# One pool for all 4 KB tiles, decay matrices per head, and another order of the mixing's steps

## The chip, the cores and the metric

The kernel runs on one core of a Trainium2 chip. The metric is the device time of one execution in microseconds. The engines are TensorE (PE in the profile; PEld is its weight load), VectorE (DVE), ScalarE (ACT), GpSimd (POOL) and SyncE (SP), which here issues all DMAs. Each engine takes its instructions in the order in which the program gives them.

## The reference

Two layers work on 256 latent and 256 context tokens of width 1024. Each layer is a half-step feed-forward, a token mixing, and another half-step feed-forward, each with a modulated norm before it and a modulated residual behind it. Cut to what matters:

```python
for l in range(DEPTH):                                    # 2
    m = split(silu(c) @ w_mod[l] + b_mod[l], 9)           # and mc from c_ctx
    x  = x  + 0.5 * m[2]  * swiglu(modulate(rms_norm(x),  m[0],  m[1]),  ffn1_w_in[l], ffn1_w_out[l])
    xc = xc + 0.5 * mc[2] * swiglu(...)                   # the context, same weights
    y, y_ctx = token_mixing(...)                          # w_in: 1024 -> 2560, three head groups
    x  = x  + m[5] * (y @ w_out[l])
    x  = x  + 0.5 * m[8] * swiglu(..., ffn2_w_in[l], ffn2_w_out[l])
    # context likewise, in the first layer alone
# token_mixing: A neighbourhood attention, 8 heads of 32, one softmax over window and context keys
#               B retention, 4 heads, q and k of 64, v of 128, both directions, decay per direction
#               C diagonal complex state-space scan, 16 groups of 64 states, both directions, GELU, GLU
```

All is float32. The result must agree with float32 products, so a product of two float32 matrices is made from three products of a rounded part (hi) and a rest (lo).

## The kernel before

Activations lie transposed, 128 features by 512 tokens (context first), eight tiles `x`. A weight comes by DMA into a 4 KB tile `raw` (128 x 1024); ScalarE rounds it into `whi`, VectorE subtracts into `wlo` (`unit`), and three matmuls per pair of tiles collect into a PSUM bank (`mm3`). A feed-forward goes through 22 blocks of hidden features in four parts. Its projections, and those of the mixing, are bound to nothing but weights and the normalised input `hhi`, `hlo`.

The mixing (`mixing`) makes the projection `ub` and then steps three generators: `s` is the state-space group (`s5`: products `s5z`, work on VectorE and GpSimd, products `s5y`), `a` the attention (`attention`: values `va`, then for each half of four heads the projections `qk` and their norm, copies that stack hi and lo parts into `qs` and `ks`, and for each token tile and head the score matmul `sc`, a maximum `mx` on VectorE, the exponential `p` on ScalarE, transposes `pt`, their copy `pts`, and the products `ot`), and `r` the retention (`retention`, `ret_head`: projections `rqk`, values `vb`, gates `rgate`, products `rab`, `rot`, `rsb`). The string `ORDER` says in which order the steps are recorded.

The program is then ordered by a planner in the file itself (`Sched.run`): each engine takes the recorded instruction of the lowest number that can start by the planner's own times, if its output tile has a free slot and no older work would be left without one (`fits`). So the number of slots of each pool and the recorded order decide which matmuls stand between a score matmul and its transposes. Names may have a limit on tiles in use (`LIMITS`: two `sc`, two `pt`).

Slots before: 55 pages of 2 KB (`page`), and 4 KB tiles by kind: three `raw`, two `whi`, two `wlo`, two `wmod` (weights of the modulation, whose rows VectorE multiplies with the row `crow` of the condition), four `ptab` (tables of the scan). The rows `crow` stay for the whole program. `h` and the mixed `y` take pages for hi and lo.

Of the kernel before, what the change touches and what calls it, by code (L numbers as in the profile page):

```python
# [21 lines left out]
ND = D // 128  # L22
# [157 lines left out]
class Sched:  # L180
# [28 lines left out]
    def record(self, eng, key, method, a, k):  # L209
# [315 lines left out]
class Block:  # L525
    NPAGES, NRAW, NHI, NLO, NMOD, AHEAD, NEAR, MODNEAR, FIRST, MOD, TAB, CUT = 55, 3, 2, 2, 2, 1000, 250, 700, 300, 0, 900, 2
    ORDER = ["saar" + "sar" * 4 + "ra" + "sar" * 4 + "g" + "rrr",
             "saar" + "sar" * 2 + "sr" * 2 + "ra" + "sar" * 2 + "sr" * 2 + "g" + "rrr"]
# [4 lines left out]
    LIMITS = dict(s5z=1, s5y=1, sc=2, pt=2, glu=2, nabias=2, rkt=1, rab=1, qs=4, ks=4)  # L533

    def __init__(self, tc, ctx, I, O):
# [14 lines left out]
        tagged(wp, "raw", self.NRAW)  # L550
        tagged(wp, "whi", self.NHI)
        tagged(wp, "wlo", self.NLO)
        tagged(wp, "ptab", 4)
        tagged(wp, "wmod", self.NMOD)
# [4 lines left out]
    def page(self, name, dtype=F32):  # L559
        return self.limited(self.nc.tile("page", [128, 512], dtype, name))  # L560

# [22 lines left out]
    def raw(self, src, n=1024):  # L584
        t = self.nc.tile("raw", [128, 1024], F32, "raw")
# [3 lines left out]
    def unit(self, src, n=1024, w=128, pages=False, at=None):  # L589
# [5 lines left out]
        for o in range(0, n, 512) if pages else (0,):  # L595
            if pages:
                m, t = 512, [self.page("raw"), self.page("whi", F32R), self.page("wlo", F32R)]
            else:
                m = n
                t = [nc.tile(x, [128, 1024], y, x) for x, y in (("raw", F32), ("whi", F32R), ("wlo", F32R))]  # L600
            r, hi, lo = [x[:, :m] for x in t]
# [21 lines left out]
    def begin(self):  # L623
# [11 lines left out]
        nc.vector.memset(self.ones, 1.0)  # L635
        self.mhalf = self.keep([128, 64], "mhalf")
# [52 lines left out]
    def mod_rows(self):  # L689

        nc = self.nc
        self.crow = self.keep([128, 2, 1024], "crow")
        self.junk = self.keep([128, 1024], "junk", mybir.dt.bfloat16)
        for r in range(2):
            for hf in range(2):
# [4 lines left out]
                nc.scalar.copy(self.crow[:, r, hf * 512:(hf + 1) * 512], b)  # L700

    def mod(self, l, ch):
# [4 lines left out]
        for d in range(ND):  # L707
            w = self.nc.tile("wmod", [128, 1024], F32, "wmod")
            nc.sync.dma_start(w, self.I["w_mod"][l, ch, d]).near = self.MODNEAR
            for r in range(n):  # L710
                nc.vector.scalar_tensor_tensor(self.junk, w, 1.0, self.crow[:, r], op0=ALU.mult, op1=ALU.mult,
# [27 lines left out]
    def norm(self, l, sh, streams):  # L739
# [3 lines left out]
        tiles = [[self.page("nu") for d in range(ND)], [self.page("hhi", F32R) for d in range(ND)],  # L743
                 [self.page("hlo", F32R) for d in range(ND)]]
        for lsl, last in self.sq_last:
# [14 lines left out]
            for d in range(ND):  # L760
                u, hh, hl = [t[d] for t in tiles]
# [9 lines left out]
        return [(tiles[1][d][:, al], tiles[2][d][:, al]) for d in range(ND)]  # L771
# [36 lines left out]
    def ffn(self, l, which, sh, streams, after, hooks={}, first=False):  # L808
# [5 lines left out]
        for ip, (f0, f1) in enumerate(PARTS):  # L814
# [3 lines left out]
            for f in range(f0, f1):  # L818
                acc = []
                for ab in range(2):  # L820
# [5 lines left out]
                    acc.append(a)  # L826
                s = self.page("fs")
                nc.scalar.activation(s[:, :n], acc[0][:, :n], AF.Silu)
                nc.vector.tensor_tensor(s[:, :n], acc[1][:, :n], s[:, :n], op=ALU.mult)
                gh = self.page("ghi", F32R)  # L830
                gl = self.page("glo", F32R)
# [49 lines left out]
    def s5_discretize(self):  # L881
# [6 lines left out]
        def new(name):  # L888
            return self.keep(S, name)
        dt = self.vexp(raw[:, 2], S)  # L890
        ar = new("s5ar")
        V.tensor_scalar(ar, raw[:, 0], -1e-4, None, op0=ALU.min)
        ai = raw[:, 1]
        th = new("s5th")
        xr = new("s5xr")
# [7 lines left out]
        k = new("s5k")  # L903
# [9 lines left out]
        q = new("s5q")  # L913
        V.tensor_tensor(q, th, th, op=ALU.mult)
        sn = new("s5sn")
        cs = new("s5cs")
# [8 lines left out]
        ph = (new("s5c"), new("s5s"))  # L925
# [12 lines left out]
        ph2 = (new("s5c2"), new("s5s2"))  # L938
# [9 lines left out]
        den = new("s5den")  # L948
        t = new("s5t")
# [4 lines left out]
        nr = new("s5nr")  # L954
# [8 lines left out]
        t3 = new("s5t3")  # L963
# [5 lines left out]
    def s5_tables(self, l):  # L969
# [112 lines left out]
        for tl in range(2):  # L1082
            for d in range(2):
                P = nc.tile("ptab", [128, 2, 4, 128], F32, "s5p")
# [125 lines left out]
    def put_y(self, y, i, src):  # L1210
        hi = self.page("yhi", F32R)
        lo = self.page("ylo", F32R)
        n = src.shape[-1]
        self.split(src, hi[:, :n], lo[:, :n])
# [511 lines left out]
```

## Time and profile before

| | us |
|---|---|
| median of 3 runs (1875.93 to 1880.08) | 1877.32 |
| the profiled execution, its own time | 1888.44 |
| its span, first to last instruction | 1886.7 |
| TensorE busy | 1797.6 (95%) |
| VectorE busy | 1327.3 (70%) |
| ScalarE busy | 668.2 (35%) |
| DMA, mean share of the 16 engines | 44.2% |

The share of TensorE is high almost everywhere. The page's forty slices show 9 of 10 or more in nearly all of them; the lower ones are the first, slices 10 to 13 (the first layer's mixing, from about 410 to 690 us) and 32 to 35 (the second's, 1460 to 1690). The granted clock is 0.973 on the mean and falls in those same slices. All instructions have one line, since a helper records them, so they are told apart by the names of their tiles.

### The profile page before, as it was taken

To read this page: it belongs to the slowest core of one execution; us is meant where nothing else is said; L and a number is where in the kernel's file an instruction comes from. 1 tells how busy PE (TensorE), PEld (TensorE's weight loads), DVE (VectorE), ACT (ScalarE), POOL (GpSimd) and SP (SyncE) were. 2 spreads that over 40 slices of the span, in tenths; PEclk is the share of its full clock that TensorE was granted. 3 is DMA by queue.
4 is the path that set the end of the run, shared out by engine and by line. 5 is a ranking of instruction groups with operands and counts; after the bars stand their busy time and mean duration, and the time that the engine had idled before them with its cause. 6 is when DMAs were issued, how large, how long until landed. Compare 5 with 4: busy or idle time off the path is not lost. (4 is left out here: it accounts for less than half of the span.)

```text
span 1886.7 us, 27751 instructions
## 1 busy us (share of the span) xinstructions
PE 1797.6 (95%) x10342; PEld 1543.3 (82%) x10342; DVE 1327.3 (70%) x2899; ACT 668.2 (35%) x1231; POOL 162.3 (9%) x226
## 2 busy tenths in 40 slices
PE   7999999999688899999999999999999979989999
PEld 5788788788567699888888898888889868779998
DVE  4999999976476897489958474547345657866565
ACT  4425222334242423222222352322233433345443
POOL 0000000022123120000000100000001223310000
PEclk9999999999699999999999999999999988989999
DMA  9444477733213442362626334438242232236665
GB/s 368 125 125 136 125 234 216 247 112 89 74 40 101 135 134 92 106 211 87 192 90 224 111 124 133 147 110 265 88 141 82 77 107 86 69 101 183 180 179 164
DMA packets 89512, 264.53 MB, mean 140 GB/s; under 512 B 11297, under 2 KB 13473, under 8 KB 89377
## 3 DMA queue, kind: packets, MB, share of 16 engines
q1 hardware_dynamic: 89376, 262.76, 44.2%
q8 instruction: 81, 1.33, 0.3%
q14 instruction: 55, 0.44, 0.1%
HBM read 254.33 MB, written 1.05 MB: 135 GB/s over the span
## 5 line engine op out<-in xcount | busy, mean ns | idle before, releaser
L522 ACT CAST whi<-raw 128x1024 fp32r<-128x1024 f32 (+3 forms) x446 | 351.0, 808 | 817.8 <-PE facc L522 664.3
L522 PE MATMUL facc<-hhi,wlo 128*128 128x512 f32 (+1 forms) x1472 | 524.8, 357 | 3.0 <-DVE wlo L522 3.0
L522 PE MATMUL facc<-hhi,whi 128*128 128x512 f32 (+1 forms) x1472 | 524.7, 358 | 2.7 <-ACT hhi L522 1.7
L522 PE MATMUL facc<-hlo,whi 128*128 128x512 f32 (+1 forms) x1472 | 525.0, 357 | 0.0
L522 DVE TENSOR_TENSOR wlo<-raw,whi 128x1024 fp32r<-128x1024 f32 (+3 forms) x446 | 402.8, 922 | 151.4 <-ACT whi L522 144.7
L522 PEld LDWEIGHTS facc<-hhi,whi 128*128 128x128 f32 x1472 | 279.8, 190 | 44.8 <-ACT hhi L522 2.7
L522 PEld LDWEIGHTS facc<-hhi,wlo 128*128 128x128 f32 x1472 | 279.8, 190 | 44.1 <-DVE wlo L522 4.9
L522 PEld LDWEIGHTS facc<-hlo,whi 128*128 128x128 f32 x1472 | 279.9, 190 | 40.8 <-issue 2.0
L522 DVE SCALAR_TENSOR_TENSOR junk<-wmod,crow 128x1024 bf16<-128x1024 f32 x224 | 274.8, 1227 | 35.6 <-DMA wmod<-in_w_mod 33.6
L522 PE MATMUL facc<-ghi,whi 128*128 128x512 f32 (+1 forms) x776 | 268.0, 347 | 3.2 <-ACT ghi L522 2.8
L522 PE MATMUL facc<-ghi,wlo 128*128 128x512 f32 (+1 forms) x776 | 268.3, 346 | 1.3 <-DVE wlo L522 1.3
L522 PE MATMUL facc<-glo,whi 128*128 128x512 f32 (+1 forms) x776 | 267.8, 346 | 0.3 <-DVE glo L522 0.3
L522 DVE SCALAR_TENSOR_TENSOR x<-facc,mcol,x 128x256 f32<-128x256 f32 x248 | 112.6, 479 | 84.0 <-PE facc L522 83.8
L522 PEld LDWEIGHTS facc<-ghi,whi 128*128 128x128 f32 x776 | 146.6, 189 | 23.0 <-ACT ghi L522 4.0
L522 PEld LDWEIGHTS facc<-ghi,wlo 128*128 128x128 f32 x776 | 146.8, 189 | 20.2 <-DVE wlo L522 2.5
L522 PEld LDWEIGHTS facc<-glo,whi 128*128 128x128 f32 x776 | 146.9, 189 | 19.1 <-DVE glo L522 1.3
L522 DVE TENSOR_TENSOR fs<-facc,fs 128x512 f32<-128x512 f32 (+1 forms) x88 | 54.7, 622 | 116.5 <-PE facc L522 115.6
L522 POOL TENSOR_TENSOR sqacc<-sqacc,sq 128x256 f32<-128x256 f32 (+1 forms) x50 | 44.8, 895 | 945.1 <-ACT sq L522 934.3
L522 ACT CAST ghi<-fs 128x512 fp32r<-128x512 f32 (+1 forms) x88 | 49.7, 566 | 55.1 <-DVE fs L522 54.5
L522 ACT ACTIVATE hhi<-nu,mcol 128x256 fp32r<-128x256 f32 x88 | 39.2, 502 | 57.8 <-DVE nu L522 57.8
L522 PE MATMUL pt<-first,p 128*128 128x128 f32 x160 | 35.7, 328 | 22.2 <-ACT p L522 19.3
L522 DVE TENSOR_TENSOR glo<-fs,ghi 128x512 fp32r<-128x512 f32 (+1 forms) x88 | 54.4, 618 | 0.2
(280 smaller groups left out, 2324.7 us busy)
## 6 DMA issues: line engine op xcount, KB each, us to landing
raw<-in_f_in SPq DMA_DIRECT2D x172, 512.0 KB, 3.7
wmod<-in_w_mod SPq DMA_DIRECT2D x128, 512.0 KB, 4.3
raw<-in_f_out SPq DMA_DIRECT2D x96, 384.0 KB, 3.2
raw<-in_w_t SPq DMA_DIRECT2D x28, 512.0 KB, 4.0
wmod<-in_w_mod SPq DMA_DIRECT2D x32, 256.0 KB, 5.4
raw<-in_f_out SPq DMA_DIRECT2D x32, 256.0 KB, 4.2
raw<-in_w_out SPq DMA_DIRECT2D x10, 512.0 KB, 3.6
raw<-in_w_vb SPq DMA_DIRECT2D x8, 512.0 KB, 3.7
```

The source lines that it names most:

```text
L522: getattr(getattr(self.nc, o.eng), o.method)(*a, **k)
```

## The change

It replaces the pools of 4 KB tiles by one of 23 slots (`pair`), from which `raw`, `whi`, `wlo` and `wmod` take tiles up to their old numbers (now `LIMITS`), as do the scan's tables, `crow`, `h` and `y` (hi and lo are halves of one tile). Pages are 40. Tiles of the first weights have names of their own (`eraw`, `ehi`, `elo`). The rows `crow` are made twice: at the start, and again for the second and later feed-forwards. Short-lived constants of `s5_discretize` share eight buffers (`brief`). The retention's decay matrices (`rd`, `rg`) are made head by head and pair by pair. Two memsets are bound to a matmul ahead of them. Scores are made over 96 stacked rows instead of 128 (the product of the two rests is left out). `ORDER` is another. In the planner, the change of matmul form that it counts looks only at whether more than 64 rows are used.

```diff
-            op.mode = (views[1][1].shape[0], op.strip is None)
+            op.mode = (views[1][1].shape[0] > 64, op.strip is None)
...
-    NPAGES, NRAW, NHI, NLO, NMOD, AHEAD, NEAR, MODNEAR, FIRST, MOD, TAB, CUT = 55, 3, 2, 2, 2, 1000, 250, 700, 300, 0, 900, 2
-    ORDER = ["saar" + "sar" * 4 + "ra" + "sar" * 4 + "g" + "rrr",
-             "saar" + "sar" * 2 + "sr" * 2 + "ra" + "sar" * 2 + "sr" * 2 + "g" + "rrr"]
+    NPAGES, NPAIRS, AHEAD, NEAR, MODNEAR, FIRST, MOD, TAB, CUT = 40, 23, 1000, 250, 700, 300, 0, 900, 2
+    ORDER = ["aarsarssarrasrsarasarsarsarsargrrr", "rasarsarsasrsrrasraarsrssrgrrr"]
...
-    LIMITS = dict(s5z=1, s5y=1, sc=2, pt=2, glu=2, nabias=2, rkt=1, rab=1, qs=4, ks=4)
+    LIMITS = dict(s5z=1, s5y=1, sc=2, pt=2, glu=2, nabias=2, rkt=1, rab=1, qs=4, ks=4, raw=3, whi=2, wlo=2,
+                  wmod=2)
...
-        tagged(wp, "ptab", 4)
-        tagged(wp, "wmod", self.NMOD)
+        tagged(wp, "pair", self.NPAIRS)
...
+    def parts(self, name):
+
+        t = self.pair(name, F32R)
+        return t[:, :512], t[:, 512:]
...
-        self.crow = self.keep([128, 2, 1024], "crow")
+        self.crow = [self.pair("crow") for r in range(2)]
...
-        tiles = [[self.page("nu") for d in range(ND)], [self.page("hhi", F32R) for d in range(ND)],
-                 [self.page("hlo", F32R) for d in range(ND)]]
+        tiles = [self.parts("h") for d in range(ND)]
...
-        hi = self.page("yhi", F32R)
-        lo = self.page("ylo", F32R)
+        y[i] = [t[:, :n] for t in self.parts("y")]
+        self.split(src, *y[i])
...
-                for st, (hi, lo, al), parts in ((qT, qn[0], (0, 0, 1, 1)), (kT, qn[1], (0, 1, 0, 1))):
+                for st, (hi, lo, al), parts in ((qT, qn[0], (0, 0, 1)), (kT, qn[1], (0, 1, 0))):
...
-        Dm = []
-        for h in range(4):
-            d = self.page("rd")
-            V.tensor_scalar(d, pa, self.lg[:, l, 0, h:h + 1], None, op0=ALU.mult)
-            V.scalar_tensor_tensor(d, pb, self.lg[:, l, 1, h:h + 1], d, op0=ALU.mult, op1=ALU.add)
-            A.activation(d, d, AF.Exp)
-            Dm.append(d)
...
-                        G.memset(t[other], 0.0)
+                        G.memset(t[other], 0.0).deps.append(made)
...
+        dm = self.page("rd")
+        V.tensor_scalar(dm, pa, self.lg[:, l, 0, hd:hd + 1], None, op0=ALU.mult)
+        V.scalar_tensor_tensor(dm, pb, self.lg[:, l, 1, hd:hd + 1], dm, op0=ALU.mult, op1=ALU.add)
+        A.activation(dm, dm, AF.Exp)
...
+        if i == 1:
+            b.later(b.MOD)
+            b.mod_rows()
+            b.later(0)
```

How this moves instructions shows on TensorE in the first half of the attention in the first layer. Before, in its context tiles (`vb` are products for the retention's values, `sc` scores, `pt` transposes of the exponentials, `ot` their products with the values, `rsw` a product of the retention):

```order
L522 MATMUL vb<-whi,hlo 128x256
L522 MATMUL sc<-ks,qs 128x256
L522 MATMUL pt<-first,p 128x128 x2
L522 MATMUL sc<-ks,qs 128x256
L522 MATMUL pt<-first,p 128x128 x2
L522 MATMUL sc<-ks,qs 128x256
L522 MATMUL pt<-first,p 128x128 x2
L522 MATMUL ot<-pts,vap 32x128 x8
```

And now, on TensorE at the same place, around the third of those scores:

```order
L522 MATMUL sc<-ks,qs 128x256
L522 MATMUL pt<-first,p 128x128 x2
L522 MATMUL vb<-whi,h 128x256
L522 MATMUL vb<-wlo,h 128x256
L522 MATMUL vb<-whi,h 128x256 x2
L522 MATMUL vb<-wlo,h 128x256
L522 MATMUL vb<-whi,h 128x256 x2
L522 MATMUL vb<-wlo,h 128x256
L522 MATMUL vb<-whi,h 128x256 x2
L522 MATMUL sc<-ks,qs 128x256
L522 MATMUL pt<-first,p 128x128 x2
```

Matmuls for the retention's values now stand between scores and transposes, and the transposes are those of an earlier score.

On TensorE a little later, in the latent tiles of the same heads, before (`qk` is the projection for the next half of the heads):

```order
L522 MATMUL sc<-ks,qs 128x512
L522 MATMUL pt<-first,p 128x128 x4
L522 MATMUL sc<-ks,qs 128x512
L522 MATMUL pt<-first,p 128x128 x4
L522 MATMUL sc<-ks,qs 128x512
L522 MATMUL pt<-first,p 128x128 x4
L522 MATMUL sc<-ks,qs 128x512
L522 MATMUL pt<-first,p 128x128 x4
L522 MATMUL qk<-hhi,whi 128x512
L522 MATMUL ot<-pts,vap 32x128 x16
```

And now there (`rgate` is the projection for a head's gate):

```order
L522 MATMUL sc<-ks,qs 128x512
L522 MATMUL rgate<-h,whi 128x512
L522 MATMUL rgate<-h,wlo 128x512
L522 MATMUL rgate<-h,whi 128x512 x2
L522 MATMUL pt<-first,p 128x128 x4
L522 MATMUL rgate<-h,wlo 128x512
L522 MATMUL rgate<-h,whi 128x512 x2
L522 MATMUL rgate<-h,wlo 128x512
L522 MATMUL rgate<-h,whi 128x512 x2
L522 MATMUL rgate<-h,wlo 128x512
L522 MATMUL pt<-first,p 128x128 x2
L522 MATMUL sc<-ks,qs 128x512
```

The gate projection, which stood ahead of this place in one piece, is now spread over it.

## Rows read from the trace of the kernel before

**Rows 1.** The page: busy us (share of the span) and instructions, TensorE
```profile
PE 1797.6 (95%) x10342; PEld 1543.3 (82%) x10342; DVE 1327.3 (70%) x2899; ACT 668.2 (35%) x1231; POOL 162.3 (9%) x226
```

**Rows 2.** Stretches, feed-forward: us, PE, PEld, DVE, ACT, POOL busy (count), PEclk, DMA, GB/s
```profile
188.70:235.90 47.20, 44.72 (x192) 35.22 (x192) 46.65 (x105) 13.38 (x27) 0.00 (x0) 1.00 0.41 125
...
943.40:990.60 47.20, 47.20 (x210) 39.09 (x209) 27.26 (x37) 13.96 (x18) 0.00 (x0) 1.00 0.28 90
```

**Rows 3.** Stretches, the four blocks from the first sc to the last pt
```profile
481.30:547.10 65.80, 47.13 (x240) 33.64 (x240) 40.39 (x124) 20.74 (x64) 15.97 (x28) 0.71 0.16 52
586.50:643.40 56.90, 45.74 (x303) 35.66 (x302) 41.57 (x133) 22.37 (x67) 16.83 (x27) 0.88 0.30 91
1521.00:1562.50 41.50, 28.15 (x173) 22.82 (x171) 25.38 (x77) 16.48 (x45) 11.35 (x17) 0.76 0.30 86
1600.30:1630.60 30.30, 26.73 (x192) 22.61 (x191) 25.55 (x88) 14.01 (x42) 11.10 (x18) 0.90 0.32 95
```

**Rows 4.** Chain's end, then timelines of PE at the full clock: start, us, what
```profile
1697.14 174.89 PE facc L522 x1454
...
526.52 1.05 PE L522 MATMUL s5y<-s5x,s5e 128*128 128x128 f32 x8
527.41 0.39 PE L522 MATMUL s5y<-u,s5t 128*128 128x128 f32 x2
...
1614.12 0.38 PE L522 MATMUL pt<-first,p 128*128 128x128 f32 x2
1614.34 0.51 PE L522 MATMUL rvar<-ones,rgt 128*128 128x1 f32 x4
```

**Rows 5.** Waits, PE's and SyncE's queue's: who for whom, us, times, longest
```profile
PE pt L522 <- ACT p L522: 19.3, 11, 3.5
...
PE sc L522 <- DMA ks<-qklo: 1.1, 2, 0.6
...
SPq L522 <- PE ot L522: 60.4, 5, 27.6
```

**Rows 6.** Timeline of PE, context tiles: start, us, what [idle before <-releaser]
```profile
484.20 0.38 PE L522 MATMUL sc<-ks,qs 128*128 128x256 f32 x1
487.56 0.64 PE L522 MATMUL pt<-first,p 128*128 128x128 f32 x2 [2.97 <-ACT p L522]
488.72 0.58 PE L522 MATMUL sc<-ks,qs 128*128 128x256 f32 x1 [0.52 <-ACT pts L522]
490.60 0.69 PE L522 MATMUL pt<-first,p 128*128 128x128 f32 x2 [1.30 <-ACT p L522]
491.87 0.58 PE L522 MATMUL sc<-ks,qs 128*128 128x256 f32 x1 [0.57 <-DVE pts L522]
493.83 0.69 PE L522 MATMUL pt<-first,p 128*128 128x128 f32 x2 [1.39 <-ACT p L522]
```

**Rows 7.** Timeline of PE, a latent tile
```profile
1531.37 0.80 PE L522 MATMUL sc<-ks,qs 128*128 128x512 f32 x1 [0.73 <-ACT pts L522]
1534.06 0.96 PE L522 MATMUL pt<-first,p 128*128 128x128 f32 x3 [1.89 <-ACT p L522]
```

**Rows 8.** Timeline of VectorE beside the first of rows 6
```profile
484.15 1.23 DVE L522 TENSOR_TENSOR wlo<-raw,whi 128x1024 fp32r<-128x1024 f32 x1
...
485.63 1.22 DVE L522 TENSOR_TENSOR wlo<-raw,whi 128x1024 fp32r<-128x1024 f32 x1
```

**Rows 9.** A stretch in a block: all instructions, then those of pt alone
```profile
1600.30:1616.00 15.70, 15.70 (x119) 14.54 (x117) 12.65 (x40) 6.06 (x18) 7.47 (x11) 1.00 0.38 101
...
1600.30:1616.00 15.70, 2.22 (x12) 1.44 (x12) 1.37 (x2) 0.59 (x1) 1.00 0.38 101
```

**Rows 10.** Timeline of SyncE in the start
```profile
31.77 6.42 SPq L522 DMA_DIRECT2D wmod<-in_w_mod  x10
```

**Rows 11.** Timeline of PE in the start, a change to column tiles
```profile
33.35 0.39 PE L522 MATMUL facc<-hhi,whi 128*128 128x512 f32 x1
33.67 0.64 PE L522 MATMUL modacc<-wmod,sc 128*32 128x128 f32 x16
```

More of the change, by code (lines that the diff above doesn't have):

```diff
@@ L560, in page, with pair @@
         return self.limited(self.nc.tile("page", [128, 512], dtype, name))
+    def pair(self, name, dtype=F32):
+        return self.limited(self.nc.tile("pair", [128, 1024], dtype, name))
+    def parts(self, name):
+        t = self.pair(name, F32R)
+        return t[:, :512], t[:, 512:]
     def bank(self, name):
@@ L584, in raw @@
     def raw(self, src, n=1024):
-        t = self.nc.tile("raw", [128, 1024], F32, "raw")
+        t = self.pair("raw")
         self.nc.sync.dma_start(t[:, :n], src)
@@ L596, in unit @@
             if pages:
-                m, t = 512, [self.page("raw"), self.page("whi", F32R), self.page("wlo", F32R)]
+                m, r, hi, lo = 512, self.page("eraw"), self.page("ehi", F32R), self.page("elo", F32R)
             else:
                 m = n
-                t = [nc.tile(x, [128, 1024], y, x) for x, y in (("raw", F32), ("whi", F32R), ("wlo", F32R))]
-            r, hi, lo = [x[:, :m] for x in t]
+                r, hi, lo = [self.pair(x, y)[:, :m] for x, y in (("raw", F32), ("whi", F32R), ("wlo", F32R))]
             nc.sync.dma_start(r, src[:, o:o + m])
@@ L707, in mod @@
         for d in range(ND):
-            w = self.nc.tile("wmod", [128, 1024], F32, "wmod")
+            w = self.pair("wmod")
             nc.sync.dma_start(w, self.I["w_mod"][l, ch, d]).near = self.MODNEAR
             for r in range(n):
-                nc.vector.scalar_tensor_tensor(self.junk, w, 1.0, self.crow[:, r], op0=ALU.mult, op1=ALU.mult,
+                nc.vector.scalar_tensor_tensor(self.junk, w, 1.0, self.crow[r], op0=ALU.mult, op1=ALU.mult,
                                                accum_out=m[:, d, r:r + 1])
@@ L760, in norm @@
             for d in range(ND):
-                u, hh, hl = [t[d] for t in tiles]
+                hh, hl = tiles[d]
+                u = self.page("nu")
                 for r_, sl in streams:
@@ L770, in norm @@
         al = slice(streams[0][1].start, streams[-1][1].stop)
-        return [(tiles[1][d][:, al], tiles[2][d][:, al]) for d in range(ND)]
+        return [(hh[:, al], hl[:, al]) for hh, hl in tiles]
     def mms(self, a, w, h, pieces):
@@ L826, in ffn @@
                     acc.append(a)
+                gh = self.page("ghi", F32R)
+                gl = self.page("glo", F32R)
                 s = self.page("fs")
@@ L889, in new, with brief @@
             return self.keep(S, name)
+        def brief():
+            return self.small(S, "s5v", bufs=8)
         dt = self.vexp(raw[:, 2], S)
-        ar = new("s5ar")
+        ar = brief()
         V.tensor_scalar(ar, raw[:, 0], -1e-4, None, op0=ALU.min)
         ai = raw[:, 1]
-        th = new("s5th")
-        xr = new("s5xr")
+        th = brief()
+        xr = brief()
         V.tensor_tensor(xr, dt, ar, op=ALU.mult)
@@ L946, in s5_discretize @@
             self.php[1 << j] = o
-        den = new("s5den")
-        t = new("s5t")
+        den = brief()
+        t = brief()
         V.tensor_tensor(den, ar, ar, op=ALU.mult)
@@ L953, in s5_discretize @@
         V.reciprocal(den, den)
-        nr = new("s5nr")
+        nr = brief()
         V.tensor_scalar(nr, pw[:, 0, 1], -1.0, None, op0=ALU.add)
@@ L962, in s5_discretize @@
         V.tensor_tensor(fr, fr, den, op=ALU.mult)
-        t3 = new("s5t3")
+        t3 = brief()
         V.tensor_tensor(t3, nr, ai, op=ALU.mult)
@@ L1083, in s5_tables @@
             for d in range(2):
-                P = nc.tile("ptab", [128, 2, 4, 128], F32, "s5p")
+                P = self.pair("s5p").rearrange("p (r q n) -> p r q n", r=2, q=4)
                 qs = slice(4 * tl, 4 * tl + 4)
@@ L1424, in retention @@
                 b = self.proj(l, 6 + 2 * p + i, h, tl, "rqk")
+                made = nc.ops[-1].i
                 s = 0.125 if i else 1.0
```

62 lines of the change are left out of this document (27 added, 35 removed).

## The prediction

> **What bounds the kernel now.** I read the page first, then the stretches of time, then who waits for whom, then the order of time around the longest waits. The page says that TensorE is busy for 1797.6 of 1886.7 us [rows 1]. The reader should see that this share is an average of two regimes. In the feed-forward stretches the engine has nothing to give: 210 matmuls of 512 columns fill 47.2 of 47.2 us, 0.225 each; even where VectorE is full (46.7 of 47.2 us) TensorE is busy for 44.7 [rows 2]. The idle time lies in the mixing, and there in four blocks, one for each half of the attention heads of each layer, from the first score matmul to the last transpose of the half. I marked them by the names sc and pt: 65.8, 56.9, 41.5 and 30.3 us, 194.5 together, with TensorE busy for 147.8 [rows 3]. So 46.7 of the kernel's 89.1 us of idle TensorE are in a tenth of its time, and the granted clock falls there to a mean of 0.71, 0.88, 0.76 and 0.90 (a mix of its two levels, 2.4 and 1.2 GHz), where the feed-forward runs at 1.00.
>
> How much work is in a block? Matmuls that follow each other at the full clock start 0.12 us apart with 256 columns in fp32r (1454 in 174.9 us), 0.225 with 512 [rows 2], 0.11 for a pass over 128 columns in fp32 (the 8 of 526.52; two passes to an instruction, and twice that with 256 columns), and 0.11 for a transpose (the 2 of 1614.12) [rows 4]. With these prices the instructions that the order puts into the four blocks are worth 30.8 + 35.9 + 19.5 + 22.1 = 108.3 us. The blocks thus last 86.2 us longer than their work: 46.7 idle, and 39.5 in which matmuls run at the lower clock or drain before a wait.
>
> What ends the idle time is one chain: a score matmul (sc), a maximum on VectorE, an exponential on ScalarE, and the transposes of the result (pt) on TensorE. It leads the list of waits, 19.3 us [rows 5]. In time it reads: the score matmul at 488.72, its transposes at 490.60, the next score at 491.87, its transposes at 493.83, with nothing between them [rows 6]. Free of queues this chain takes 1.9 us for a context tile, and 2.7 for a latent tile (1531.37 to 1534.06) [rows 7]. With a queue it takes longer: for the score matmul of 484.20 it took 3.4 us, because VectorE had a weight split of 1.23 us ahead of the maximum and another one ahead of its sign change [rows 8].
>
> **The change part by part.** *Order of the mixing.* The order shows how far the transposes of a head stand behind its score matmul, in TensorE work at the prices above. Before, 21 of the 48 heads have less work there than the free chain takes, 21.5 us short in all; now one head has, 0.6 us short. What fills the place are the matmuls of the retention's values (vb), its gates (rgate), and the q and k projections. Free chains alone therefore give back 20.9 us of the 46.7.
>
> The other 25.8 us are queues on VectorE and ScalarE, and shorter chains of the other two head groups. More cover helps there too: the median distance grows from 2.7 to 3.5 us, by 0.8. But VectorE has not less to do: it is busy for 132.9 us in the blocks [rows 3], with 384 instructions from the first maximum to the last of each, against 341 now, which at the same mean is 118 us for 110.1 us of TensorE work (38.7 + 33.5 + 20.9 + 17.0, the new blocks). Both engines are then nearly full, and a chain between two full engines meets queues. I keep between two thirds and all of the 25.8, so 17 to 26 us, and take 22 with the rest of the free chains. The lower clock and the drains go with the idle time, 39.5 / 46.7 = 0.85 us for each, so the excess becomes 22 x 1.85 = 41 us, and the blocks give back 86 - 41 = **45 us**. Bounds: 5 us of idle left gives 77; all 25.8 left gives 38; if the lower clock stays although the idle time goes, 46.7 - 22 = 25.
>
> *Half of the rows for half of the clock?* The stretch of 1600.3 to 1616.0 holds 12 transposes and a granted clock of 1.00 [rows 9]. The Trainium skill (TensorE: Matmul & The Clock Gate, Part 4: PE-mode transpose) says that transposes don't count as activity for the clock, so that blocks full of them would stay slow without any wait; by it the clock part would not come back and the sum would be 25 us. By the row the filled block ran at full clock, so I take it as part of a rival.
>
> *One pool for the 4 KB tiles, 55 pages cut to 40.* Counts of the weight tiles stay at 3, 2 and 2, so the weight stream keeps its depth; a tile now takes the slot that was free longest, which can only shorten a wait that the plan did not foresee. SyncE waits much (60.4 us for ot alone [rows 5]), but ahead of use. I put 0, from -3 to +3; what pages could cost is a rival below.
>
> *The rows of c made again (crow).* 16 transposes more, 16 x 0.11 = 1.8 us. They stand where the first mixing begins and TensorE may wait for the normalised input anyway, but I count all of it: +1.8, and 0 at best.
>
> *Start.* The last four loads of the first modulation now wait for pages and go behind two modulation weights, the table of constants and a weight tile. The ten loads before took 6.4 us of SyncE's queue [rows 10]; four issues in front make about 2.6 us. What is queued behind is the next weight tile, and TensorE waits for both. In the order 30 matmuls of 512 columns stand ahead of the last modulation steps, 6.8 us of cover. I put 0, with -2 to +3.
>
> *Tables of the second layer's scan.* Their last products move on VectorE from the first layer's second feed-forward into the second layer's first: 24 instructions. The nearest bound is the stretch with VectorE full, in which TensorE lost 2.5 us [rows 2]. 0, up to +2.5.
>
> *Decay matrices per head, memsets bound to the matmul ahead, short-lived constants, y in one tile.* The instructions are the same, only later; the decay pair (two on VectorE, one exponential) is hidden under the head's gate projection, 24 matmuls. 0 to +2.
>
> *Scores over 96 rows instead of 128.* 48 matmuls with as many columns, and 32 small copies fewer on SyncE. The trace has no matmul over 96 rows. The gain is at most the waits for those copies, 1.1 us [rows 5]. Against: a change of tile form. The nearest rows are a matmul of 512 columns and the column tiles behind it, 33.35 to 33.67: 0.32 us instead of 0.225 [rows 11], so 0.1 for a change of form and 9.6 for 96. I take 0, since all columns of the array stay in use; both ends are in the range.
>
> **Sum.** Against the profiled execution, 1888.4 us with its surroundings (span 1886.7): 1888.4 - 45 + 1.8 = 1845.2. The profiled run is 11.1 us over the median of the shown runs (1877.3). Less that, the forecast is **1834 us**; with idle left of 17 to 26 us it is 1824 to 1841, and with the small terms 1818 to 1850.
>
> **The rivals.** (a) *The queues vanish too.* The spread-out projections cover them all and 5 us of idle stay: gain 77, 1802 us. For it: in the stretch 1600.3 to 1616.0 VectorE is busy for 12.65 of 15.7 us, 81%, and TensorE for all of it at the full clock [rows 9]. Against it: 118 us for VectorE beside 110. (b) *VectorE or the clock takes over.* Either the clock part stays (gain 25), or VectorE sets the pace: at 81% its 118 us would last 146, at 70%, about what it reaches now (68%), 168, a gain of 26. Both give about 1853. (c) *The plan moves and the time doesn't*, within 0.2% (3.8 us, about what a measurement of this kernel can tell): the filled places were late for another reason, for instance the copies of k; the list of waits gives those only 1.1 us. 1877. (d) *Slower: pages.* Each head writes two pages, the exponentials and their transposes, 96 in all, and with 15 slots fewer a slot comes round sooner, so that ScalarE's write waits for the last reader, and weight casts queue behind it. SyncE's copies of bias tiles already wait so, up to 27.6 us for one ot [rows 5]. At 0.25 us for each tile, stretched by 1.85, this is 44 us and eats the gain; at 0.4 it is 71 and the kernel takes about 1905 (1834 + 71). The Trainium skill speaks for it (Perfetto Trace Analysis, Optimization Strategy): the same gap repeating "can mean there isn't enough SBUF/PSUM for the next tile to be allocated", and pages shrink by 30 KB a partition. Against it in this trace: the repeated gaps are ended by the chain's exponential, 19.3 us [rows 5].
>
> **How the numbers follow.** Chances: forecast 0.56, (a) 0.20, (b) 0.14, (c) 0.04, (d) 0.06. The range 1803 to 1860 takes in the forecast, (b), and half of (a). Faster 0.90, same 0.04, slower 0.06.
>
> **What would show it.** In the trace after: the four blocks by sc and pt should last about 151 us (110 + 41) where they lasted 194.5, the wait of pt for p should fall from 19.3 to under 8 us, the clock in the blocks should rise over 0.9, VectorE in them should pass 75% of the time (68% before), and the feed-forward stretches should stay as they are. I am wrong if the blocks still hold 40 us of idle, if ScalarE waits for TensorE before writing p or pts, if score matmuls take longer than before at the full clock, or if the start or the first feed-forward loses more than 5 us.

## The result and the profile after

The changed kernel takes 1804.94 us, the median of 4 runs (1802.62 to 1808.15), against 1877.74 for the kernel before in the same session: ratio 0.9613, 95% interval 0.9594 to 0.9631. It is 72.8 us faster; the forecast was 1834, so 29 us of gain were not foreseen, and the time is near that of rival (a), 1802. The profiled execution has a span of 1803.5 us, 1805.3 with its surroundings.

The page of the kernel after, TensorE's line: busy us (share of the span), instructions.

```profile
PE 1759.7 (98%) x10358; PEld 1525.2 (85%) x10358; DVE 1314.2 (73%) x2899; ACT 658.2 (36%) x1234; POOL 164.7 (9%) x226
```

Compared with [rows 1], TensorE is idle for 43.8 us where it was idle for 89.1, and its busy time, which counts slow-clock matmuls too, fell by 37.9 us although 16 transposes were added. The four blocks of [rows 3] in the kernel after (us, PE, PEld, DVE, ACT, POOL busy, granted clock, DMA share, GB/s), and their sum:

```profile
475.90:522.80 46.90, 42.87 (x303) 35.35 (x302) 38.47 (x126) 25.99 (x73) 12.98 (x21) 0.96 0.28 89
552.80:590.50 37.70, 36.85 (x311) 32.26 (x310) 35.70 (x124) 22.27 (x68) 14.61 (x26) 1.00 0.27 89
1468.20:1491.30 23.10, 22.78 (x190) 20.13 (x190) 22.13 (x75) 13.47 (x40) 3.82 (x8) 1.00 0.37 117
1527.70:1547.00 19.30, 18.28 (x165) 16.84 (x166) 18.18 (x69) 10.24 (x36) 5.38 (x10) 1.00 0.15 54
sum 127.00, PE 120.78 PEld 104.58 DVE 114.47 ACT 71.98 POOL 36.79; mean PE 30.19 PEld 26.14 DVE 28.62 ACT 17.99 POOL 9.20
```

194.5 us became 127.0, TensorE is idle for 6.2 of them instead of 46.7, the clock is 0.96 to 1.00 instead of 0.71 to 0.90, and VectorE, busy for 68% before, is busy for 90%. Who waits for whom, TensorE's rows for scores and transposes (us, times, longest), to be read against [rows 5]:

```profile
PE pt L522 <- ACT p L522: 1.9, 4, 0.6
...
PE sc L522 <- ACT p L522: 1.4, 2, 1.0
...
PE sc L522 <- DMA ks<-qklo: 0.7, 1, 0.7
```

The wait that led the list fell from 19.3 to 1.9 us. In order of time, TensorE in the first context tile (start, us, what), where [rows 6] had nothing between a score and its transposes:

```profile
479.29 0.29 PE L522 MATMUL sc<-ks,qs 96*128 96x256 f32 x1
479.42 0.38 PE L522 MATMUL pt<-first,p 128*128 128x128 f32 x2
479.55 0.36 PE L522 MATMUL sc<-ks,qs 96*128 96x256 f32 x1
479.76 0.38 PE L522 MATMUL pt<-first,p 128*128 128x128 f32 x2
479.90 0.36 PE L522 MATMUL vb<-whi,h 128*128 128x256 f32 x1
480.10 0.28 PE L522 MATMUL vb<-wlo,h 128*128 128x256 f32 x1
480.21 0.40 PE L522 MATMUL vb<-whi,h 128*128 128x256 f32 x2
```

The transposes behind a score are those of an earlier one, and the retention's values (vb) fill the time until the next are ready. From here on I call **excess** what a block (first score to the end of the last transpose) lasts beyond its matmuls at the prices of [rows 2, 4]. Before it is 87.6 us of 146.9 lost in the whole kernel; after it is 11.3 of 62.0.

### The profile page after: what moved, and what is told of

It reads as the page before. It is cut to its first block, busy times and chain, and to the rows that moved or that the text cites. A ratio compares the mean times of both kernels' runs of the same rounds, so it can differ in the third digit from the quotient of the medians.

```text
span 1803.5 us, 27673 instructions
## 1 busy us (share of the span) xinstructions
PE 1759.7 (98%) x10358; PEld 1525.2 (85%) x10358; DVE 1314.2 (73%) x2899; ACT 658.2 (36%) x1234; POOL 164.7 (9%) x226
## 4 chain that ended last, share of the span: by engine, by line
PE 73%; DVE 6%; issue 1%; ACT 1%; DMA 1%; SPq 1%; POOL 0%; POOLq 0%; ACTq 0%; DVEq 0%
PE facc L522 59%; PE qk L522 2%; PE rqk L522 2%; PE vb L522 2%; PE va L522 1%; DVE wlo L522 1%; PE ub L522 1%; DVE gel L522 1%; SPq L522 1%; PE rgate L522 1%; PE rot L522 1%; PE s5y L522 1%; PE glu L522 1%; PE pt L522 1%; PE s5z L522 0%
## 5 line engine op out<-in xcount | busy, mean ns | idle before, releaser
L522 PE MATMUL facc<-h,whi 128*128 128x512 f32 (+1 forms) x2880 | 772.2, 356 | 3.4 <-ACT h L522 2.4
L522 PEld LDWEIGHTS facc<-h,whi 128*128 128x128 f32 x2880 | 511.3, 190 | 80.9 <-ACT h L522 2.9
L522 PE MATMUL facc<-h,wlo 128*128 128x512 f32 (+1 forms) x1440 | 509.9, 355 | 2.5 <-DVE wlo L522 2.5
L522 PEld LDWEIGHTS facc<-h,wlo 128*128 128x128 f32 x1440 | 272.8, 190 | 41.2 <-DVE wlo L522 3.4
L522 PE MATMUL facc<-glo,whi 128*128 128x512 f32 (+1 forms) x632 | 227.8, 361 | 1.2 <-DVE glo L522 1.2
L522 PE MATMUL facc<-ghi,whi 128*128 128x512 f32 (+1 forms) x632 | 227.1, 361 | 1.6 <-ACT ghi L522 1.6
L522 PE MATMUL facc<-ghi,wlo 128*128 128x512 f32 (+1 forms) x632 | 227.7, 361 | 0.2
L522 POOL TENSOR_TENSOR sqacc<-sqacc,sq 128x256 f32<-128x256 f32 (+1 forms) x50 | 46.7, 936 | 1142.3 <-ACT sq L522 1141.4
L522 PEld LDWEIGHTS facc<-ghi,whi 128*128 128x128 f32 x632 | 119.5, 189 | 20.3 <-ACT ghi L522 2.5
L522 ACT ACTIVATE fs<-facc 128x512 f32<-128x512 f32 (+1 forms) x88 | 47.8, 544 | 176.8 <-PE facc L522 176.8
L522 ACT ACTIVATE h<-nu,mcol 128x256 fp32r<-128x256 f32 x88 | 39.6, 501 | 38.2 <-DVE nu L522 36.0
L522 ACT ACTIVATE sq<-x 128x256 f32<-128x256 f32 (+1 forms) x66 | 29.0, 451 | 59.6 <-DVE x L522 38.0
L522 PE MATMUL vb<-whi,h 128*128 128x256 f32 x256 | 50.7, 288 | 0.0
```

Source lines behind the costliest of these rows:

```text
L522: getattr(getattr(self.nc, o.eng), o.method)(*a, **k)
```

## Experiments

All twelve are shown; e10 and e12 are one run each. "Short" is what the order of a kernel lacks between scores and transposes against the free chains of 1.9 and 2.7 us, summed over the 48 heads, as in the prediction; it is worked out from the program, not read from a trace. Excess is given for the four blocks and in sum. The kernel after was not timed again beside the experiments. The kernel before was, and its median moved from 1877.7 to between 1879.9 and 1880.8 us in the sessions of e1 to e11, so a difference from after is uncertain by some 3 us.

| kernel | median us | short us | excess us, blocks 1 to 4 | sum |
|---|---|---|---|---|
| before | 1877.7 | 21.5 | 35.1, 21.0, 23.0, 8.5 | 87.6 |
| e10 before, second profile | 1877.7 | 21.5 | 35.1, 19.2, 21.5, 8.7 | 84.5 |
| e2 new order, old pools | 1859.4 | 16.5 | 22.4, 20.3, 20.9, 6.7 | 70.3 |
| e4 the pool alone | 1855.2 | 16.8 | 32.4, 1.3, 23.3, 2.6 | 59.6 |
| e5 free memsets | 1838.8 | 10.1 | 20.6, 1.6, 17.3, 0.6 | 40.1 |
| e1 old order | 1825.6 | 6.3 | 19.6, 1.2, 4.1, 0.5 | 25.5 |
| e3 128 rows | 1811.2 | 6.2 | 16.2, 1.4, 2.5, 1.5 | 21.7 |
| after | 1804.9 | 0.6 | 7.4, 1.4, 1.3, 1.3 | 11.3 |
| e7 copies on ScalarE | 1813.1 | 1.0 | 7.7, 1.4, 0.4, 1.0 | 10.4 |
| e8 copies on VectorE | 1814.1 | 0.7 | 13.8, 3.1, 2.9, 1.5 | 21.2 |
| e6 decay up front, 21 slots | 1875.2 | 0.5 | 1.7, 0.9, 1.7, 1.4 | 5.6 |
| e9 21 slots | 1876.7 | 0.3 | 5.2, 1.7, 1.6, 1.4 | 10.0 |
| e12 free memsets, 20 slots | 2165.5 | 4.8 | 15.6, 9.1, 1.6, 0.8 | 27.0 |
| e11 searched order | 1794.4 | 0.6 | 3.8, 1.3, 0.6, 0.8 | 6.5 |

### Which edit fills the places?

The prediction put the whole gain under "order of the mixing". The first theory to be tried was that it doesn't matter which edit puts work between scores and transposes; the rival, that the strings do it.

**e1**, the old strings in the changed kernel:

```diff
-    ORDER = ["aarsarssarrasrsarasarsarsarsargrrr", "rasarsarsasrsrrasraarsrssrgrrr"]
+    ORDER = ["saar" + "sar" * 4 + "ra" + "sar" * 4 + "g" + "rrr",
+             "saar" + "sar" * 2 + "sr" * 2 + "ra" + "sar" * 2 + "sr" * 2 + "g" + "rrr"]
```

> The changed kernel with the two old strings of ORDER and all else as changed. Cover theory: what counts is the TensorE work that the plan puts between a score matmul and its transposes, whichever edit puts it there. In the order of this kernel 10 of the 48 heads have less work there than the free chain takes (1.9 us context, 2.7 us latent), 6.2 us short in all; before it was 21 heads and 21.5 us, after 1 head and 0.6 us. The traces give 86 us of excess in the four blocks for 21.5 us short and 12 us for 0.6, so about 3.5 us for each us short: excess 12 + 3.5 x 5.6 = 32 us, time 1805 + 20 = 1825 us (1815 to 1840). Rival, the strings do it: the old strings bring the old time back, less what the decay and pools give, 1865 to 1880 us. Rival, only pools and no order: same as after, 1805 us.

Measured: 1825.64 us, ratio 0.9716 (0.9696 to 0.9736). The strings are worth 20.7 us of the 72.8 when the rest is there (19 by the ratios).

**e2**, the new strings in the kernel before. Its old 55 pages are too few for that order, so it has 56, and two edits of the change go along to save others: the short-lived constants and the decay matrices per head.

```diff
-    NPAGES, NRAW, NHI, NLO, NMOD, ... = 55, 3, 2, 2, 2, ...
+    NPAGES, NRAW, NHI, NLO, NMOD, ... = 56, 3, 2, 2, 2, ...
...
+    ORDER = ["aarsarssarrasrsarasarsarsarsargrrr", "rasarsarsasrsrrasraarsrssrgrrr"]
...
+        def brief():
+            return self.small(S, "s5v", bufs=8)
...
+        dm = self.page("rd")
```

> The kernel before with the new strings of ORDER and its old pools (h and y in pages). It needs 56 pages for that, and has them by taking from the changed kernel the decay matrices per head and the eight short-lived buffers; scores over 128 rows. Cover theory: 15 heads are short by 16.5 us in its order, so excess 12 + 3.5 x 15.9 = 68 us against 86: 18 us gained, 1860 us (1845 to 1872). Rival, the strings do it: nearly the whole gain, 1805 to 1820 us. Rival, the pools alone do it: 1878 us, as before.

Measured: 1859.37 us, ratio 0.9895 (0.9877 to 0.9912). The strings bring 18 to 20 us here, with the decay matrices per head; all four blocks keep most of their excess.

**e4**, the pool alone, without the new strings, the decay per head, the bound memsets and the 96 rows:

```diff
-    NPAGES, NRAW, NHI, NLO, NMOD, ... = 55, 3, 2, 2, 2, ...
+    NPAGES, NPAIRS, ... = 40, 23, ...
...
+        tiles = [self.parts("h") for d in range(ND)]
...
+        y[i] = [t[:, :n] for t in self.parts("y")]
```

> The kernel before with the one pool of 23 slots and 40 pages (h and y leave the pages, crow made twice, the eight short-lived buffers), with the old strings, decay matrices up front, 128 rows and unbound memsets. Cover theory: 12 heads short by 16.8 us, excess 12 + 3.5 x 16.2 = 69 us, gain 17 us, about 1861 us (1845 to 1872). Rival (d) of the prediction, 15 slots fewer cost waits: 1880 to 1905 us. Rival, the pool alone makes the gain: 1805 to 1815 us.

Measured: 1855.23 us, ratio 0.9881 (0.9858 to 0.9903): 22 to 25 us gained by an edit that the prediction priced at 0, and no sign of rival (d). Smaller edits of the change go along that are not in the cut: the eight short-lived buffers, `crow` made twice, the planner's rule of form, the pages of a feed-forward's products (`ghi`, `glo`) taken before that of its gate (`fs`), and in the second layer one page for the `qs` of two heads. None of these was tried alone. The stretches of its four blocks say where:

```profile
478.39:543.09 64.70, 45.89 (x249) 32.86 (x250) 41.84 (x130) 21.34 (x66) 16.00 (x28) 0.76 0.18 54
584.79:619.65 34.86, 34.14 (x288) 29.67 (x287) 33.44 (x119) 19.93 (x64) 10.02 (x19) 1.00 0.42 128
1496.20:1539.46 43.26, 30.79 (x180) 24.35 (x179) 25.65 (x80) 16.02 (x45) 10.40 (x17) 0.73 0.24 83
1577.13:1600.19 23.06, 21.50 (x187) 18.66 (x188) 22.70 (x77) 12.67 (x39) 11.46 (x18) 1.00 0.32 98
```

The second halves are cured, at the full clock, while the first halves are about as before (32.4 and 23.3 us of excess). So the change has at least two parts in this, and the second theory is one of **room**: the plan starts a matmul early only if the tiles that it and its readers need have slots. Before, `h` held 16 of the 55 pages and `y` up to 16 more as the mixing went on, which left 39 down to 23; now there are 40 with neither in them.

**e5**, the memsets unbound:

```diff
-                        G.memset(t[other], 0.0).deps.append(made)
+                        G.memset(t[other], 0.0)
...
-            G.memset(st, 0.0).deps.append(nc.ops[-2].i)
+            G.memset(st, 0.0)
```

> The changed kernel with its two memsets (of the unused halves of the retention's k tiles and of its state tile) no longer bound to the matmul ahead of them. They depend on nothing then, so the plan starts them early and each holds a page from then on. Room theory (the pages that are free while a half of the heads runs decide how many foreign matmuls the plan can put between scores and transposes): 8 heads are short by 10.1 us in its order, all in the first halves (5.4 in the first layer, 4.7 in the second, 0 in the second halves). At 3.5 us of excess for each us short the first and third block gain 19 and 16 us of excess, the other two stay at 1 to 2 us: 1805 + 33 = 1838 us (1825 to 1848). Rival, GpSimd's memsets are hidden and cost nothing: 1805 us. Rival, they were a cost at the head of GpSimd's queue and are better early: 1800 us.

Measured: 1838.75 us, ratio 0.9782 (0.9761 to 0.9803), with 20.6 and 17.3 us of excess in the first halves and 1.6 and 0.6 in the second. The timelines of the second layer show pages held. First GpSimd and ScalarE in e5 (tiles cleared, and where they are written for use; a tile is used in the order in which it was cleared):

```profile
1416.16 0.53 POOL L522 MEMSET rst<- 128x512 f32 x1 [0.80 <-PE facc L522]
1418.26 0.52 POOL L522 MEMSET rqk<- 64x512 f32 x1
1449.32 0.52 POOL L522 MEMSET rqk<- 64x512 f32 x1
1482.95 0.53 POOL L522 MEMSET rst<- 128x512 f32 x1 [12.97 <-PE pt L522]
...
1518.60 0.37 ACT L522 COPY rst<-rsb 64x256 f32<-64x256 f32 x1 [0.79 <-PE rsb L522]
...
1547.97 0.75 ACT L522 ACTIVATE rqk<-rqk 64x256 f32<-64x256 f32 x2
1594.77 0.76 ACT L522 COPY rst<-rsb 64x256 f32<-64x256 f32 x2 [4.12 <-PE rsb L522]
```

Then the same tiles in the kernel after:

```profile
1491.04 0.53 POOL L522 MEMSET rst<- 128x512 f32 x1
1524.32 1.10 POOL L522 MEMSET rqk<- 64x512 f32 x2
...
1491.70 0.76 ACT L522 COPY rst<-rsb 64x256 f32<-64x256 f32 x2 [1.02 <-PE rsb L522]
1525.14 0.77 ACT L522 ACTIVATE rqk<-rqk 64x256 f32<-64x256 f32 x2
```

In e5 three pages, and from 1483 on four, lie unused through the whole third block (1479.3 to 1514.3), each for about 100 us or more before its use; bound to the matmul, they are cleared less than 1 us before they are written. The memsets themselves take 0.5 us each. In the first layer the early tiles (cleared at 399 and 402, written at 463) are in use when the first block begins at 469.9, and the next is cleared at 492, when 13 of the block's 20 us are lost; so there the held pages don't explain the loss.

**e12** asks whether it is the page that counts. It is e5 with six pages more (and three 4 KB slots fewer, which ruins the time elsewhere, so the blocks alone are read):

```diff
-    NPAGES, NPAIRS, ... = 40, 23, ...
+    NPAGES, NPAIRS, ... = 46, 20, ...
```

> The run with unbound memsets again, with 46 pages instead of 40 (and 20 slots of 4 KB instead of 23, which will cost much ahead of the mixing; so not the whole time counts here but the four blocks). Room theory: up to six tiles (two k tiles and a state tile for each of two pairs of heads) are cleared early and each holds a page; with six pages more this no longer keeps foreign matmuls out of the first halves. In the order of this kernel the third block is short by 0 us (4.7 with 40 pages) and the first by 2.1 (5.4): excess in the third block 1 to 2 us (17 with 40 pages), in the first 7 to 11 us (21 with 40 pages). Rival, the early memsets cost by their place in GpSimd's queue and not by pages: 17 and 21 us again.

Measured: excess 15.6 and 9.1 us in the first layer, 1.6 and 0.8 in the second; 2165.46 us in all. The third block did what the room theory says (17.3 to 1.6), although four of its pages lie cleared and unused from its start at 1833.5 to its end at 1856.6. First GpSimd, then where ScalarE writes the first of them (the others follow at 1890 and 1922):

```profile
1353.67 0.53 POOL L522 MEMSET rst<- 128x512 f32 x1 [1.48 <-issue]
1488.40 1.10 POOL L522 MEMSET rqk<- 64x512 f32 x2 [134.20 <-PE facc L522]
1517.65 0.53 POOL L522 MEMSET rst<- 128x512 f32 x1 [28.15 <-issue]
...
1857.08 0.76 ACT L522 COPY rst<-rsb 64x256 f32<-64x256 f32 x2 [0.96 <-PE rsb L522]
```

So it isn't the early clearing that costs, but the lack of pages: 36 or 37 of 40 were left by the cleared tiles in e5's third block, 42 of 46 here, all 40 in the kernel after. Fewer slots alone don't change this block (1.6 us of excess in e9). The first block fell from 20.6 to 15.6 only, above the 7 to 11 expected, and the second got worse. With 20 slots for `h`, `y` and weights the plan is another one in other ways too, so the first layer settles nothing: for the third block the room theory is shown, for the first it stays open.

**e3**, scores over 128 rows:

```diff
-                for st, (hi, lo, al), parts in ((qT, qn[0], (0, 0, 1)), (kT, qn[1], (0, 1, 0))):
+                for st, (hi, lo, al), parts in ((qT, qn[0], (0, 0, 1, 1)), (kT, qn[1], (0, 1, 0, 1))):
...
-                    nc.tensor.matmul(sc[:, :nk * 128], qT[:96, (q4 - ... kT[:96, :nk * 128],
+                    nc.tensor.matmul(sc[:, :nk * 128], qT[:, (q4 - ... kT[:, :nk * 128],
```

> The changed kernel with scores over 128 stacked rows again (the product of the two rests is back, and 32 small copies on SyncE). If the 96 rows only spare copies: 1805 to 1808 us. If a tile of 96 rows costs a change of form (9.6 us by the bound of the prediction): 1795 us. Cover theory: the copies that the plan must place move it, 5 heads are short by 6.2 us in its order where it was 1 and 0.6, so 1805 + 20 = 1825 us (1810 to 1830).

Measured: 1811.18 us, ratio 0.9639 (0.962 to 0.9657), 6 us slower than after by the medians and 5 by the ratios, whose intervals just overlap. The feared change of form isn't there as a cost: the 96 rows gain, if anything. The excess moved from 7.4 to 16.2 in the first block alone, where its order is short by 5.8 us; 20 us were expected for that, 6 came.

### What else the pool is worth

**e6**, the decay matrices up front again, which wants more pages, so that there are 44 of them and 21 slots:

```diff
+        Dm = []
+        for h in range(4):
+            d = self.page("rd")
...
-        dm = self.page("rd")
+        dm = tabs[0][hd]
```

> The changed kernel with the decay matrices made up front again: six pages are held through the retention, and so that the program fits the pages go from 40 to 44 and the 4 KB slots from 23 to 21. Room theory: 4 pages more against 6 held, 3 heads short by 0.5 us in its order, so the time of after: 1805 us (1800 to 1812). Rival, making them per head puts VectorE's work where it is covered, and up front it stands in the way: 6 matrices, 8 VectorE instructions of about 0.6 us and 8 exponentials for each layer, 5 to 10 us: 1810 to 1815 us. Rival, 21 slots of 4 KB are too few for the weights: over 1815 us.

Measured: 1875.2 us, ratio 0.9979 (0.9964 to 0.9994), far off every expectation but the last. The blocks are the best of all (5.6 us of excess). The loss lies ahead of them, and the edit had two causes in it, so e9 takes one away.

**e9**, the slots of e6 with nothing else:

```diff
-    NPAGES, NPAIRS, ... = 40, 23, ...
+    NPAGES, NPAIRS, ... = 44, 21, ...
```

> Control for the run with decay up front: the changed kernel with 44 pages and 21 slots of 4 KB, and nothing else changed (decay matrices per head). If the 4 KB slots made that loss (they hold 8 tiles of h, 2 of crow, 4 tables, 3 raw, 2 whi, 2 wlo and 2 wmod in the first feed-forward, 23 in all): 1875 us (1865 to 1885), lost from 235 to 475 us, in the first feed-forward and the norm of the first mixing, with 1 to 2 us of excess in each block. If the decay matrices up front made it: 1805 us (1800 to 1812).

Measured: 1876.73 us, ratio 0.998 (0.9969 to 0.9991). So it was the slots, and decay up front costs nothing that these runs can show. A stretch of e9 at the norm of the first mixing, VectorE's costliest group there (us busy, mean ns), and the longest wait on TensorE:

```profile
445.20:488.30 43.10, 17.39 (x66) 14.14 (x65) 39.00 (x78) 8.82 (x21) 12.91 (x9) 0.56 0.26 80
```
```profile
L522 DVE SCALAR_TENSOR_TENSOR junk<-wmod,crow 128x1024 bf16<-128x1024 f32 x21 | 26.7, 1270 | 2.6 <-DMA wmod<-in_w_mod 2.4
```
```profile
488.18 0.80 PE L522 MATMUL ub<-h,whi 128*128 128x256 f32 x2 [12.61 <-ACT h L522]
```

With two slots fewer the weights of the modulation come late, and 21 of their rows, 26.7 us of VectorE, fall between the feed-forward and the input of the mixing. In the kernel after none of them stands there. Some 38 of the 72 us are lost in this stretch and the matmuls behind it, and most of the rest in the feed-forward ahead of it, where TensorE waits 11.1 us for rests of weights (`wlo`) on VectorE. The first feed-forward wants all 23: eight of `h`, two of `crow`, four tables, three `raw`, and two each of `whi`, `wlo` and `wmod`.

### Is VectorE the limit at 90%?

**e7** and **e8** move copies of the transposed exponentials from one engine to the other:

```diff
-                    if (q4 + hh) % 2:
+                    if True:                 # e7: all on ScalarE
+                    if False:                # e8: all on VectorE
                         A.copy(pt[:, :nk * 128], tb[:, :nk * 128])
```

> The changed kernel with all copies of the transposed exponentials (pts) on ScalarE; VectorE had every second one, 24 in all, about 0.45 us each, so some 11 us leave VectorE in the four blocks (114 us busy of 127). Theory that VectorE is full but not the limit, since the plan's cover takes its queue in: 6 heads short by 1.0 us, time as after, 1806 us (1800 to 1811). Rival, VectorE sets the pace of the blocks (rival b of the prediction): 5 to 10 us come back, 1795 to 1800 us.

> The opposite: all 48 copies of the transposed exponentials on VectorE, 24 more of about 0.45 us, 11 us, so VectorE's work in the four blocks rises from 114 to about 125 us where the blocks last 127. Theory that the plan takes the queue in (3 heads short by 0.7 us): 1806 us (1802 to 1813). Rival, VectorE sets the pace (it needs its time over 0.9 of its share): 125 / 0.9 = 139 us for the blocks, 1817 us.

Measured: 1813.13 us (ratio 0.9648, 0.9625 to 0.967) and 1814.1 us (0.9653, 0.9633 to 0.9673). Both are slower than after, by 8 and 9 us (7 and 8 by the ratios), and neither as either theory says. In e7 the blocks have the excess of after (10.4), so VectorE's 11 us were not missing there; what was lost is one wait between the blocks, TensorE for VectorE, which itself was held until a DMA (start, us, what, idle before):

```profile
553.75 0.42 DVE L522 TENSOR_TENSOR s5rc<-s5rw,s5p 128x256 f32<-128x256 f32 x1 [8.55 <-DMA ks<-qklo]
```
```profile
555.37 1.22 PE L522 MATMUL rot<-ram,vc 128*128 128x256 f32 x2 [7.80 <-DVE ram L522]
```

In e8 the excess nearly doubles, to about 20 us, 13.8 of them in the first block. Its first two blocks:

```profile
475.43:523.99 48.56, 40.98 (x273) 33.38 (x272) 41.06 (x129) 20.60 (x61) 10.46 (x20) 0.89 0.22 69
560.75:597.75 37.00, 36.33 (x296) 30.68 (x294) 35.97 (x123) 17.43 (x56) 14.53 (x26) 1.00 0.30 88
```

VectorE is busy for 97% of the second block, and TensorE is idle for 0.7 us of it (the 3.1 us of excess in the table fall below 2 if its two `glu` products count with the 0.86 us that each takes at 594.25 and 595.54); the first, at 85%, loses 13.8. So the share of VectorE doesn't set the pace. What hurt in the first block are waits of TensorE for single results of VectorE: once 2.2 us for the scan (`s5rb`), and four times, 0.5 to 1.65 us each, for the copies themselves (pts), which "short" doesn't count: it looks at the chain to the exponential alone. The copies in the list of who waits for whom, over the whole kernel:

```profile
PE ot L522 <- DVE pts L522: 2.6, 2, 1.6
```

### The profile of before once more, and another order

**e10**, no edit:

> The kernel before once more, for a second profiled execution: the first one was 11 us over its median. If these 11 us were in the four blocks (the clock that the chip grants after an idle time differs from run to run), their excess is 76 instead of 86 us here and the span 1876; if they were elsewhere, the blocks have 86 us again and the loss is smaller outside them.

Measured: span 1875.9 us, 84.5 us of excess in the blocks, 51.5 of loss elsewhere (59.3 in the first profile). So most of the 11 us by which the first profile lay over its median, about 8, were outside the blocks and 3 in them, and the subtraction in the forecast was right.

**e11**, other strings in the changed kernel:

```diff
-    ORDER = ["aarsarssarrasrsarasarsarsarsargrrr", "rasarsarsasrsrrasraarsrssrgrrr"]
+    ORDER = ["arasassarrrasrsarasarrsaasrsargrrr", "rasarssasrrarsarsaarrrsssrgrrr"]
```

> The changed kernel with two other strings of ORDER, found by moving single steps and keeping what the planner's own times say is shorter (8 us by them). Cover theory: 2 heads short by 0.7 us as after (1 and 0.6), so nothing is won in the blocks, and what is won must come from the stretches between and behind them, which lose 29 us after: 1800 us (1795 to 1806). Rival, the planner's times do not reach that far: 1805 to 1810 us.

Measured: 1794.41 us (5 runs, 1791.55 to 1797.02), ratio 0.9538 (0.9516 to 0.9559), 10.5 us better than after (14 by the ratios) and so better than both kernels. Of the 8.4 us by which its loss fell, 4.8 are in the blocks, most in the first, and 3.6 outside; the expectation that nothing was left to win in the blocks was wrong.

## Why the prediction was right, and where not

**The number: in part luck.** 1804.9 lies in the stated range of 1803 to 1860, but only 2 us inside its lower end, which was set there to take in half of rival (a). The forecast's own range, 1818 to 1850, misses it, and so does the length of the blocks, 151 us forecast and 127.0 measured.

**Where the gain lies: right.** Against the second profile of before, whose span is 72.4 us over that of after, the excess of the blocks fell by 73.2 us and the loss elsewhere by 0.8, against 1.7 of added work. The whole gain is in the four blocks, as forecast.

**The size, 45 us: the step that failed** is "I keep between two thirds and all of the 25.8 ... and take 22". 22 us of idle time were to stay in the blocks, stretched to 41 of excess; 6.2 and 11.3 were measured, which is rival (a), 5 us. I had taken the part of the wait beyond the free chain as a queue that cover doesn't reach. But the queue is part of the chain that the plan covers. From the end of a score to the end of its exponential it takes 3.0 us before and 3.1 after in the median of the 48 heads: the queues did not vanish, though the longest chains, over 8 us, fell from ten to four. What grew is the priced work between a score and its transposes (the score itself not counted), from 2.5 to 3.4 us in the median. I took 3.5 us of excess for each us that the order is short, from the kernels before and after; this forecast the times of e1, e2, e4 and e5 to within 6 us. It missed e3 by 14, e7 and e8 by 7 and 8, and e6 by 70, whose loss lies outside the blocks. In the table the price runs from 1.9 (e3) to 3.7 us (e2) among the kernels that are short by more than 4 us, so it is a rough one.

**VectorE beside it: wrong as a limit.** The forecast held 118 us of VectorE beside 110 of TensorE for a meeting of two full engines. It was 114.5 in 127.0, and e8's second block runs at 97% with TensorE idle for 0.7 of 37.0 us. What did cost in e7 and e8 were single waits for VectorE, not its share.

**The clock: right.** It went with the idle time. The second block of after holds 48 transposes in 37.7 us at a granted clock of 1.00. The rule of the Trainium skill (TensorE: Matmul & The Clock Gate, Part 4: PE-mode transpose) that transposes don't count as activity gave a gain of 25 us, read as in the prediction. The trace doesn't agree with that reading; whether transposes themselves count it can't tell, since 263 of this stretch's 311 matmuls are no transposes.

**The parts: wrong in their shares.** The order as printed is the work of all edits together, and the prediction booked it to the strings. Taken away alone, the strings cost 20.7 us, the bound memsets 33.8 (priced 0 to +2), the 96 rows 6.2 (priced 0), each uncertain by some 3. Alone on the kernel before, the pool brings 22 to 25 (priced 0, -3 to +3), the strings with the decay 18 to 20. They don't add up: without the pool the new strings fit only with help, the pool alone leaves the first halves as they were, and with unbound memsets these still lose 20.6 and 17.3 us. The decay matrices were not told apart from room: up front they were tried only with four pages more (e6), where the blocks have 5.6 us of excess. The planner's rule of form and the other small edits in e4 were not tried alone.

**Rival (d), pages: the sign was wrong.** I read 55 to 40 as a loss of 15. Counted without `h` and `y` it is a gain. The rule of the Trainium skill that I set aside (Perfetto Trace Analysis, Optimization Strategy), that a repeating gap can mean a lack of room for the next tile, did name a part of the cause in the kernel before. e4's second halves agree with it: from 21.0 and 8.5 us of excess to 1.3 and 2.6 without the new order. The releaser of the gaps, the exponential, told only what ended them, not why nothing else stood there. The pool's danger was in the other kind of slot (e9).

**The small terms.** The second `crow` is there with its 16 transposes, ahead of a wait for the input (start, us, what):

```profile
419.02 1.25 PE L522 MATMUL crow<-first,sc 128*128 128x128 f32 x10
420.11 0.38 PE L522 MATMUL nrb<-first,nr 128*128 128x128 f32 x2
420.33 0.82 PE L522 MATMUL crow<-first,sc 128*128 128x128 f32 x6
421.79 0.51 PE L522 MATMUL ub<-h,whi 128*128 128x256 f32 x2 [0.65 <-ACT h L522]
```

About 1.9 us of work, and TensorE still waits 0.65 behind it, so its price is at most about the 1.8 counted. The start (up to 188.7) and the first feed-forward (to 377) stayed: against the priced work their loss moved by about 0.5 us, up and down. The scan's tables cost about 2 us, at 1053 to 1056, within the bound of 2.5. Of what would have shown me wrong, 40 us of idle didn't come. ScalarE's waits for TensorE before it writes `p` did not grow, 5.4 us in all where they were 6.7, but some are now for transposes, which the kernel before doesn't have (us, times, longest):

```profile
ACT p L522 <- PE pt L522: 2.2, 2, 1.6
```

Both are in the fourth block, whose excess is 1.3 us in all.

## What to carry to other kernels

When a planner or pools decide the order, a gap can have two causes: the work that ends it and the lack of a slot that kept other work out. Count the slots that are free for the stretch in question, after the long-lived tiles, rather than the pool's size, and look for tiles that are taken long before they are written. Judge a reordering by the work that stands between a producer and its reader against the real chain, queue included; here an engine that was 90% busy beside it was no reason to mark the gain down.

## What had not been expected of the hardware

VectorE at 97% of a 37 us stretch beside a TensorE that is busy for 36.3 of the 37.0 at the full clock (e8). And scores over 96 rows beside matmuls over 128 cost no form change that the trace shows: from the score matmul at 479.29 to the transposes at 479.76 it takes 0.47 us for two scores and two transposes, 0.46 at the prices of [rows 4]. The quickest start of a next matmul behind a score of 256 columns is after 0.120 us with 96 rows and 0.118 with 128 (e3), behind one of 512 columns after 0.232 and 0.229.
